# Pinning the first matmul of each recurrence and level step behind the matmul emitted just ahead of it

## The chip, the core and the metric

The kernel runs on one core of one Trainium2 chip. A core has five engines with a queue each, worked off in order: PE (matmuls, with its weight loads shown apart as PEld), DVE, ACT and POOL for elementwise work, and SP, which issues nearly all DMAs here. The metric is the device time of one execution in microseconds, as the median of several runs. Before the change the three runs took 3159.82, 3169.68 and 3175.28 us.

## What is computed

Two layers of a backbone over 256 latent and 256 context tokens, 2048 channels wide. The first layer is a bidirectional gated DeltaNet, the second a differential attention. Each is wrapped in RMSNorm, an adaptive shift, scale and gate, a SiLU gate and an output projection. The change lies in the DeltaNet alone, whose core in the reference is this:

```python
tinv = lax.linalg.triangular_solve(eye + lower, eye, left_side=True, lower=True, unit_diagonal=True)
u = tinv @ (vc * bc[..., None])
w = tinv @ (kb * jnp.exp(gc)[..., None])
...
def step(s, inp):
    q_i, k_i, u_i, w_i, a_i, gl_i = inp
    v_new = u_i - w_i @ s
    o_i = q_i @ s + a_i @ v_new
    s = s * gl_i[..., None, None] + jnp.einsum('bhck,bhcv->bhkv', k_i, v_new)
    return s, o_i
```

There are 16 key heads with two value heads each, in both directions. The steps of the scan depend on each other through the state `s`.

## The kernel before, in words

The 512 tokens are cut into four chunks of 128, and the work of the DeltaNet into 16 groups `g`, one for each key head, with its two value heads `h` and two directions `dd`. For each group these things run:

- **The filler** (`filler`, lines 671 to 696): six input projections (k, q, v0, v1, z0, z1) of 48 matmuls each, 128x512, with weights split in a high and a low part. Their PSUM tiles are called `pj`, and there are two. They don't depend on the recurrence, but what they write does: the tiles `sz` for z0 and z1 exist twice, and are freed when the outputs of a group are finished (`chain_fin`).
- **The levels** (`stream_lev`, lines 779 to 826; two such streams): the triangular inverse of a chunk, doubled in three levels. A level is a matmul group `iv<-T,m`, a mask on DVE that makes `R` (line 807), the group `iv<-U,R`, and, but for the last level, `iv<-R,U` and two copies on ACT (lines 824, 825).
- **The recurrence** (`steps_b`, lines 873 to 957): four steps `t` per group. A step is a chain of PE groups with an elementwise operation behind each: `sb<-S,kT` and then `y` on DVE and its cast `yb` on ACT (895 to 903); `sb<-yb,uf` and the copy `x0` (920, 922); `sb<-x0,m` and the residual `yb` (926 to 929); `sb<-yb,uf` again and `x` (933, 935); `sb<-x,kx` and the state `S` (940 to 946). The outputs are `so<-S,qT` and `so<-x,at` (907, 952).
- Beside them `stream_m` and `stream_at` (decay matrices, and a block inverse in small DVE operations, lines 736 and 738), and the pieces of the adaptive modulation on POOL and ACT.

**Who sets the order.** Two layers do. The class `Drive` (lines 521 to 563) runs these generators against a clock of its own: after each piece a generator yields the PE time it used and the latency until its next piece may be emitted, and the ready one with the lowest priority number goes next (recurrence 1, levels 1.5, the filler 9). This gives the order in which instructions are emitted. Then the framework's scheduler sets the order on each engine, by a model of when each instruction is ready: an instruction may be put ahead of ones that were emitted earlier on its engine. What it decides is fixed when the program is built; on the chip each engine takes its queue in that order.

After the loop the output projection follows in two halves of heads, tiles `woA0` to `woA15` (heads 0 to 15) and `woB0` to `woB15` (heads 16 to 31), 48 matmuls each; a head's output goes through the DRAM tensor `yd` and is loaded again as `yr`, then split into `yh` on ACT (204) and `yl` on DVE (206). The second layer comes last. All calls of `mm` appear in the profile as line 87.

Of the kernel before, what the change touches and what calls it, by code (L numbers as in the profile page):

```python
# [20 lines left out]
P = 128  # L21
# [44 lines left out]
def body(ctx, tc, D, d, out):  # L66
    nc = tc.nc
# [16 lines left out]
    wp = ctx.enter_context(pool("wp", side="right"))  # L84

    def mm(o, l, r, start=True, stop=True):
        nc.tensor.matmul(o, l, r, start=start, stop=stop)  # L87

    cs = cst.tile([P, C_MAIN], F32, name="cs")
    nc.sync.dma_start(cs, d["consts"][:, :C_MAIN])  # L90
# [182 lines left out]
    def sb():  # L273
        return psm.tile([P, 2, 2, P], F32, tag="sb", name="sb", bufs=1)

    def so():
        return psm.tile([P, 2, 2, P], F32, tag="so", name="so", bufs=1)
# [43 lines left out]
    for k0 in range(0, KT, SK):  # L321
# [12 lines left out]
        for n, src, _ in EARLY:  # L334
            w = SK * P
            r = t0.tile([P, w], F32, tag="er", name=f"e{n}r{k0}", bufs=4)
# [178 lines left out]
    def ev(*k):  # L515
        return evs.setdefault(k, Event())
# [48 lines left out]
    dr = Drive()  # L565
    LX = 1.8

    def free(k, n=1, lat=0.0):
        if lat:
            dr.add(0, later(k, n), lat)  # L570
        else:
            res[k].free += n

    def later(k, n):
        res[k].free += n
        return
        yield
# [120 lines left out]
    def quad(t):  # L698
        return t.rearrange("p (u i) -> p u i", u=4)
# [79 lines left out]
    def stream_lev(p):  # L779
        yield ev("conv", 0, "v0")  # L780
        yield ev("conv", 0, "v1")
        for g in range(G):
            for half in range(2):
                yield ev("tu", g, half)
                yield ("uf", 1)
                st = sts[g]
                c = 2 * half + p
                m16 = st["m"][half][0]
                tu = st["tu"][half]

                def t16(tag):
                    return dl.tile([P, 4, P], F16, tag=f"{tag}{p}", name=f"{tag}{g}{c}", bufs=1)

                lvb = lambda n: lv[:, n - 4].unsqueeze(1).to_broadcast([P, 4, P])
                Tm, U = t16("T"), t16("U")
                for dst, src in ((Tm, tu[0]), (U, tu[1])):
                    for dd in range(2):
                        nc.sync.dma_start(dst[:, 2 * dd:2 * dd + 2], src[p, :P, dd])
                dr.set("ld", g, half, p)
                yield 0.0, 4.0  # L800
                for n in range(4, 7):
                    last = n == 6
                    pp = iv()
                    for u in range(4):
                        mm(pp[:, u * P:(u + 1) * P], m16[:, u // 2, p, u % 2], Tm[:, u])
                    R = t16("R")
                    nc.vector.tensor_tensor(R, quad(pp), lvb(n), ALU.mult)  # L807
                    yield 0.22, 30 / 10
                    pu = iv()
                    for u in range(4):  # L810
                        mm(pu[:, u * P:(u + 1) * P], R[:, u], U[:, u])
                    if last:
                        uf = dl.tile([P, 4, P], F16, tag="uf", name=f"uf{g}{c}", bufs=8)
                        nc.scalar.copy(uf, quad(pu))
                        st.setdefault("uf", {})[c] = uf
                        yield 0.22, 1.5 * LX
                        dr.set("uf", g, c)
                    else:
                        U2 = t16("U")
                        pt = iv()  # L820
                        for u in range(4):
                            mm(pt[:, u * P:(u + 1) * P], U[:, u], R[:, u])
                        U, Tm = U2, t16("T")
                        nc.scalar.copy(Tm, quad(pt))  # L824
                        nc.scalar.copy(U, quad(pu))  # L825
                        yield 0.43, 30 / 10
# [46 lines left out]
    def steps_b(g, t, half, st, S, O):  # L873
        kT, qT, ktok, uf = st["kT"], st["qT"], st["ktok"], st["uf"]
        v = st["v"][half]
        m16, ml = st["m"][half]
        cd = (ORDER[0][t], ORDER[1][t])
        col = lambda a, dd, h: a[:, cd[dd], dd, 2 * g + h:2 * g + h + 1]
        fl = lambda a: a.rearrange("p d h i -> p (d h i)")
        f2 = lambda a: a.rearrange("p h i -> p (h i)")  # L880
        DH = [(dd, h) for dd in range(2) for h in range(2)]

        def vec(tag, dt=F32):
            return dl.tile([P, 2, 2, P], dt, tag=tag, name=f"{tag}{g}{t}", bufs=1)

        if t < 3:
            kx = vec("kx")
            for dd in range(2):
                nc.gpsimd.tensor_tensor(kx[:, dd], ktok[:, cd[dd]].unsqueeze(1).to_broadcast([P, 2, P]),
                                        kd[:, cd[dd], dd, 2 * g:2 * g + 2].unsqueeze(2).to_broadcast([P, 2, P]),  # L890
                                        ALU.mult)
        if t > 0:
            b = sb()
            for dd in range(2):
                mm(f2(b[:, dd]), kT[:, cd[dd]], f2(S[:, dd]))
            y = vec("y")
            for dd, h in DH:
                nc.vector.scalar_tensor_tensor(y[:, dd, h], b[:, dd, h], col(eg, dd, h), v[:, cd[dd] % 2, h],
                                               ALU.mult, ALU.subtract)
        else:  # L900
            y = v
        yb = vec("yb", BF16)
        nc.scalar.copy(fl(yb), fl(y))
        if t > 0:
            o1 = so()
            for dd in range(2):
                mm(f2(o1[:, cd[dd] % 2]), qT[:, cd[dd]], f2(S[:, dd]))
            for dd, h in DH:
                c = cd[dd] % 2
                if t == 2:  # L910
                    nc.scalar.activation(O[:, c, h], o1[:, c, h], AF.Copy, scale=col(eg, dd, h))
                else:
                    nc.vector.scalar_tensor_tensor(O[:, c, h], o1[:, c, h], col(eg, dd, h), O[:, c, h],
                                                   ALU.mult, ALU.add)
            yield 1.7, 2.6 * LX
        else:
            yield 0.0, 1.0 * LX
        b = sb()
        for dd, h in DH:
            mm(b[:, dd, h], uf[cd[dd]][:, 2 * dd + h], yb[:, dd, h])  # L920
        x0 = vec("x0", BF16)
        nc.scalar.copy(fl(x0), fl(b))
        yield 0.22, 1.6 * LX
        b = sb()
        for dd, h in DH:
            mm(b[:, dd, h], m16[:, dd, cd[dd] % 2, h], x0[:, dd, h], True, False)
            mm(b[:, dd, h], ml[:, dd, cd[dd] % 2, h], x0[:, dd, h], False, True)
        rb = vec("yb", BF16)
        nc.vector.tensor_tensor(fl(rb), fl(y), fl(b), ALU.subtract)  # L929
        yield 0.43, 1.8 * LX  # L930
        b = sb()
        for dd, h in DH:
            mm(b[:, dd, h], uf[cd[dd]][:, 2 * dd + h], rb[:, dd, h])
        x = vec("x")
        nc.vector.tensor_tensor(fl(x), fl(x0), fl(b), ALU.add)  # L935
        yield 0.22, 1.8 * LX
        if t < 3:
            b = sb()
            for dd, h in DH:
                mm(b[:, dd, h], kx[:, dd, h], x[:, dd, h])  # L940
            if t == 0:
                nc.vector.tensor_copy(fl(S), fl(b))
            else:
                for dd, h in DH:
                    nc.vector.scalar_tensor_tensor(S[:, dd, h], S[:, dd, h], col(egl, dd, h), b[:, dd, h],
                                                   ALU.mult, ALU.subtract)
        if t % 2 == 0:
            yield ev("at", g, half)
        at = st["at"]
        o0 = so()  # L950
        for dd, h in DH:
            mm(o0[:, cd[dd] % 2, h], at[cd[dd]][:, 2 * dd + h], x[:, dd, h])
        if t == 0:
            nc.scalar.copy(fl(O), fl(o0))
        else:
            nc.vector.tensor_tensor(fl(O), fl(O), fl(o0), ALU.subtract)
        yield (1.74 if t < 3 else 0.87), (2.2 if 0 < t < 3 else 1.0) * LX
# [93 lines left out]
    for ct in range(KT):  # L1051
        ps = pj()
        wout_tile(ps, d["wout"][0, ct], f"woA{ct}", yA, T, True, True)
        x = dl.tile([P, T], F32, tag="th", name=f"xb{ct}", bufs=2)
# [94 lines left out]
    for p in range(NP_):  # L1149
# [12 lines left out]
        for hd in range(2):  # L1162
            dh = 2 * p + hd
            spread(late_1, dh, KT // 2, 4)
            qT, kT = [], []
# [17 lines left out]
            for qt in range(2):  # L1183
# [30 lines left out]
                o = l1.tile([P, 256], F32, tag="lo", name=f"lo{dh}{qt}", bufs=2)  # L1214
# [90 lines left out]
def build(nc, arrays, D):  # L1305
    d = {n: nc.dram_tensor(f"in_{n}_dram", a.shape, mybir.dt.from_np(a.dtype), kind="ExternalInput").ap()
         for n, a in arrays.items()}
    out = nc.dram_tensor("out_0_dram", (P, D // P, 256), F32, kind="ExternalOutput").ap()
    with tile.TileContext(nc, schedule_with_timeline_sim=True) as tc:
        body(tc, D, d, out)  # L1310
# [12 lines left out]
```

## Time and profile before

| | |
|---|---|
| median of three runs | 3169.68 us (3159.82 to 3175.28) |
| the profiled execution | 3178.9 us |
| its span, first to last instruction | 3177.1 us |
| PE busy | 2847.2 us, 90% |
| DVE, POOL, ACT busy | 66%, 66%, 59% |
| mean granted TensorE clock | 0.956 |

The span is that of the profiled execution, 1.8 us less than its time. From 250 to 2000 us the groups of the DeltaNet run, with the same mix of work all along; before it lie the first norm and the first projections, behind it the output projection and the second layer. Busy time of PE is modelled from the length of each matmul, so the idle time and the spacing of starts say more than the busy share. The clock is a share of full speed: 1.0 is 2.4 GHz and 0.5 is 1.2 GHz, the only two levels.

### The profile page before, as it was taken

The page shows a single profiled execution, that of the slowest core. Times are in us where ns is not written, and L with a number is a line of the kernel's source. Part 1 is how long each engine was busy: PE and PEld are TensorE (multiplying, and loading weights), DVE is VectorE, ACT ScalarE, POOL GpSimd, SP SyncE. Part 2 cuts the span into 40 slices and gives each one's busy share as a digit, 9 for nine tenths or more (in the row PEclk, how much of TensorE's full clock was granted, in tenths as well). Part 3 has the DMA queues.
Part 4 walks back from the last instruction along what each step waited for, and adds up shares of the span by engine and source line. Part 5 has one row for each costly group of instructions (what it writes and reads, how often), then busy time and mean ns, then how long its engine had stood idle before and what let it go on. Part 6 is the DMA issues. An engine that isn't in the chain of part 4 may idle for free.

```text
span 3177.1 us, 51834 instructions
## 1 busy us (share of the span) xinstructions
PE 2847.2 (90%) x15822; PEld 2245.4 (71%) x15822; DVE 2108.5 (66%) x4475; ACT 1863.0 (59%) x5447; POOL 2086.8 (66%) x2370
## 2 busy tenths in 40 slices
PE   7777898888988988988988988899898999999998
PEld 3455676666766766766766766678686888888897
DVE  7978868768688688688688677632334654544454
ACT  4245666666766766666665765654455665634354
POOL 5877677776777777677777767566466666722234
PEclk8888999999999999999999999899999999999999
DMA  9634445555545445445455455666754555533335
GB/s 336 237 99 117 119 126 126 129 128 127 133 124 133 127 127 138 119 122 136 128 120 139 124 127 123 168 176 198 221 149 126 152 156 158 155 114 110 115 128 163
DMA packets 507183, 457.01 MB, mean 144 GB/s; under 512 B 241171, under 2 KB 383251, under 8 KB 502803
## 3 DMA queue, kind: packets, MB, share of 16 engines
q1 hardware_dynamic: 506900, 453.68, 51.4%
q8 instruction: 124, 2.03, 0.3%
q14 instruction: 157, 1.29, 0.2%
q10 hardware_dynamic: 2, 0.02, 0.0%
HBM read 427.18 MB, written 26.36 MB: 143 GB/s over the span
## 4 chain that ended last, share of the span: by engine, by line
PE 27%; DVE 11%; DMA 10%; POOL 5%; ACT 4%; issue 4%; SPq 1%; POOLq 0%; DVEq 0%; ACTq 0%
PE pj L87 24%; POOL rp L149 3%; DMA aw<-in_adaw_dram 3%; DMA gra<-gc_d 2%; DMA grm<-gc_d 2%; DVE bP L736 1%; DVE gra L711 1%; DVE grm L711 1%; ACT rp L150 1%; PE at L87 1%; PE sb L87 1%; PE iv L87 1%; DVE bY L738 1%; DMA yr<-yd 1%; DVE R L807 0%
## 5 line engine op out<-in xcount | busy, mean ns | idle before, releaser
L150 ACT ACTIVATE rp<-rp 128x256 f32<-128x256 f32 x1024 | 426.6, 417 | 397.9 <-POOL rp L149 394.0
L736 DVE TENSOR_TENSOR bP<-bX,bY 64x1 f32<-64x1 f32 (+14 forms) x480 | 226.2, 471 | 12.3 <-ACT bY L734 4.7
L150 ACT ACTIVATION_READ_ACCUMULATOR rp<-rp 128x1 f32 x1024 | 193.8, 189 | 0.0
L711 DVE TENSOR_SCALAR grm<-grm,gct,lnb 128x128 f32<-128x128 f32 x256 | 140.5, 590 | 63.3 <-DMA grm<-gc_d 62.6
L711 DVE TENSOR_SCALAR gra<-gra,gct,lnb 128x128 f32<-128x128 f32 x256 | 117.1, 500 | 84.1 <-DMA gra<-gc_d 83.6
L807 DVE TENSOR_TENSOR R<-iv,lv 128x512 f16<-128x512 f32 x192 | 127.0, 679 | 44.4 <-PE iv L87 44.0
L166 DVE CUSTOM_DVE_ANT_0 aj<-ar,crow 128x1024 bf16<-128x1024 f32 x80 | 116.1, 1452 | 10.7 <-DMA ar<-in_adaw_dram 9.5
L87 PEld LDWEIGHTS <-m 128*128 128x128 f16 x1024 | 75.8, 101 | 60.8 <-issue 53.2
L713 ACT ACTIVATE grm<-grm 128x512 f32<-128x512 f32 x64 | 40.3, 630 | 130.3 <-DVE grm L711 130.1
L738 DVE TENSOR_REDUCE bY<-bP 64x1 f32<-64x1 f32 (+14 forms) x480 | 108.8, 227 | 8.4
L769 POOL TENSOR_TENSOR ma<-ma,cs 128x512 f32<-128x512 f32 x64 | 86.2, 1346 | 24.4 <-DVE ma L719 14.8
L87 PE MATMUL iv<-U,R 128*128 128x128 f16 x768 | 76.1, 225 | 22.7 <-DVE R L807 18.6
L87 PEld LDWEIGHTS <-R 128*128 128x128 f16 x768 | 48.2, 100 | 65.2 <-DVE R L807 29.9
L713 ACT ACTIVATE gra<-gra 128x512 f32<-128x512 f32 x64 | 40.3, 630 | 84.8 <-DVE gra L711 81.4
L87 PE MATMUL iv<-T,m 128*128 128x128 f16 x768 | 73.5, 227 | 17.9 <-DMA T<-tu_d 13.1
L87 PE MATMUL sb<-yb,uf 128*128 128x128 bf16 x512 | 54.5, 225 | 39.1 <-DVE yb L929 24.0
L87 PEld LDWEIGHTS <-uf 128*128 128x128 f16 x512 | 35.4, 101 | 67.4 <-issue 59.4
L772 POOL TENSOR_TENSOR ml<-ma,m 128x512 bf16<-128x512 f32 x64 | 75.1, 1174 | 7.8 <-ACT m L771 7.7
L824 ACT CAST T<-iv 128x512 f16<-128x512 f32 x128 | 73.8, 577 | 7.8 <-PE iv L87 6.8
L87 PE MATMUL so<-x,at 128*128 128x128 f32 x512 | 74.1, 281 | 2.1 <-DVE x L935 1.8
L825 ACT CAST U<-iv 128x512 f16<-128x512 f32 x128 | 75.6, 591 | 0.0
L87 PEld LDWEIGHTS so<-x,at 128*128 128x128 f32 x512 | 66.9, 195 | 4.2 <-DVE x L935 2.2
(2767 smaller groups left out, 11567.0 us busy)
## 6 DMA issues: line engine op xcount, KB each, us to landing
aw<-in_adaw_dram SPq DMA_DIRECT2D x512, 128.0 KB, 3.0
ar<-in_adaw_dram SPq DMA_DIRECT2D x32, 1024.0 KB, 6.1
gra<-gc_d SPq DMA_DIRECT2D x128, 128.0 KB, 4.4
grm<-gc_d SPq DMA_DIRECT2D x128, 128.0 KB, 4.3
mb_d<-m SPq DMA_DIRECT2D x32, 256.0 KB, 4.5
U<-tu_d SPq DMA_DIRECT2D x128, 64.0 KB, 2.7
T<-tu_d SPq DMA_DIRECT2D x128, 64.0 KB, 2.4
yd<-sz SPq DMA_DIRECT2D x32, 256.0 KB, 2.9
```

Source lines behind the costliest of these rows:

```text
L87: nc.tensor.matmul(o, l, r, start=start, stop=stop)
L149: nc.gpsimd.tensor_tensor(pr, r, cr[:, s], ALU.mult)
L150: nc.scalar.activation(pr, pr, AF.Copy, accum_out=acc[:, s, q:q + 1])
L166: nc.vector.tensor_tensor_reduce(jk, rq, cr, 1.0, 0.0, ALU.mult, ALU.add, a)
L711: nc.vector.tensor_scalar(gr[:, u], gr[:, u], gct[:, c, dd, j:j + 1], lnb[:, c, dd, j:j + 1], ALU.subtract, ALU.min)
L713: nc.scalar.activation(gr, gr, AF.Exp)
L736: nc.vector.tensor_tensor(pr[:, :i, :i], X[:, i, :i].unsqueeze(1).to_broadcast([64, i, i]), Y[:, :i, :i].rearrange("p j c -> p c j"), ALU. ...
L738: nc.vector.tensor_reduce(Y[:, i, :i], pr[:, :i, :i], AX.X, ALU.add)
L769: nc.gpsimd.tensor_tensor(ma, ma, ident.unsqueeze(1).to_broadcast([P, 4, P]), ALU.add)
L772: nc.gpsimd.tensor_tensor(ml[:, :, k], mv, m16[:, :, k], ALU.subtract)
L807: nc.vector.tensor_tensor(R, quad(pp), lvb(n), ALU.mult)
L825: nc.scalar.copy(U, quad(pu))
```

## The change

`mm` now returns its instruction. A helper `pin` passes the first matmul (`k == 0`) of a PE group to the scheduler's `keep_in_program_order`, which adds an edge of order, without a wait, to the PE instruction emitted just before it. So the scheduler may no longer put this matmul ahead of that one. Instructions emitted later may still go ahead of the pinned one, and the other matmuls of the group have no such edge. In a level the groups `iv<-T,m` and `iv<-U,R` are pinned, in a step `sb<-S,kT`, both `sb<-yb,uf`, `sb<-x0,m` and `sb<-x,kx`.

```diff
     def mm(o, l, r, start=True, stop=True):
-        nc.tensor.matmul(o, l, r, start=start, stop=stop)
+        return nc.tensor.matmul(o, l, r, start=start, stop=stop)
...
+    def pin(k, ins):
+        return tc.keep_in_program_order(ins) if k == 0 else ins
...
-                        mm(pp[:, u * P:(u + 1) * P], m16[:, u // 2, p, u % 2], Tm[:, u])
+                        pin(u, mm(pp[:, u * P:(u + 1) * P], m16[:, u // 2, p, u % 2], Tm[:, u]))
...
-                        mm(pu[:, u * P:(u + 1) * P], R[:, u], U[:, u])
+                        pin(u, mm(pu[:, u * P:(u + 1) * P], R[:, u], U[:, u]))
...
-                mm(f2(b[:, dd]), kT[:, cd[dd]], f2(S[:, dd]))
+                pin(dd, mm(f2(b[:, dd]), kT[:, cd[dd]], f2(S[:, dd])))
...
-            mm(b[:, dd, h], uf[cd[dd]][:, 2 * dd + h], yb[:, dd, h])
+            pin(2 * dd + h, mm(b[:, dd, h], uf[cd[dd]][:, 2 * dd + h], yb[:, dd, h]))
...
-            mm(b[:, dd, h], m16[:, dd, cd[dd] % 2, h], x0[:, dd, h], True, False)
+            pin(2 * dd + h, mm(b[:, dd, h], m16[:, dd, cd[dd] % 2, h], x0[:, dd, h], True, False))
...
-            mm(b[:, dd, h], uf[cd[dd]][:, 2 * dd + h], rb[:, dd, h])
+            pin(2 * dd + h, mm(b[:, dd, h], uf[cd[dd]][:, 2 * dd + h], rb[:, dd, h]))
...
-                mm(b[:, dd, h], kx[:, dd, h], x[:, dd, h])
+                pin(2 * dd + h, mm(b[:, dd, h], kx[:, dd, h], x[:, dd, h]))
```

Two places show what this does to PE's order. The first is in group 9, from the state update of step 0 (`x90`, `kx90`) to the next step's use of the state (`S9`); `g10v0` and `g10z1` are weights of the filler for group 10, `g11q` of that for group 11. PE's rows before:

```order
L87 MATMUL pj_15740<-hhi_100,g10v0hi0256_15794 128x512
L87 MATMUL pj_15740<-hlo2_452,g10v0hi0256_15794 128x512
L87 MATMUL sb_15634<-x90_15601,kx90_15419 128x128 x4
L87 MATMUL so_15650<-x90_15601,at90_15450 128x128 x2
L87 MATMUL so_15650<-x90_15601,at91_15462 128x128 x2
L87 MATMUL pj_15740<-hhi_100,g10v0lo0256_15795 128x512
...
L87 MATMUL sb_15760<-S9_15417,kT9_13708 128x256 x2
L87 MATMUL pj_15740<-hhi_100,g10v0lo1256_15817 128x512
L87 MATMUL pj_15740<-hhi_100,g10v0hi1256_15816 128x512
```

And PE's rows now, from the last filler matmul ahead of the place to the first one behind it:

```order
L87 MATMUL pj_16678<-hhi_100,g10z1lo3256_17015 128x512
...
L87 MATMUL sb_15634<-x90_15601,kx90_15419 128x128 x4
L87 MATMUL so_15650<-x90_15601,at90_15450 128x128 x2
L87 MATMUL so_15650<-x90_15601,at91_15462 128x128 x2
L985 MATMUL so_15750<-cs_63,O81_14787 128x128 x4
L87 MATMUL sb_15760<-S9_15417,kT9_13708 128x256 x2
L87 MATMUL so_15770<-S9_15417,qT9_14277 128x256 x2
...
L595 MATMUL tr_16632<-cs_63,thg11k_16421 128x128 x4
...
L87 MATMUL pj_17046<-hhi_100,g11qhi00_17049 128x512
```

The same step stands four projections later against the filler (behind z1 of group 10, where it stood within v0), and no filler matmul is left between its parts: 56 matmuls stand there without one, from the residual of step 0 to the correction of step 1. The second place is the end of the recurrence: the transposes of the last group's last output (`O151`), which heads 30 and 31 of `woB` wait for. PE's rows before:

```order
L87 MATMUL pj_25857<-yh0_24554,woA8hi00_25860 128x512
L87 MATMUL pj_25857<-yl0_24555,woA8hi00_25860 128x512
L87 MATMUL pj_25857<-yh0_24554,woA8lo00_25861 128x512
L982 MATMUL so_24532<-cs_63,O151_24359 128x128
L87 MATMUL pj_25857<-yh1_24563,woA8hi00_25860 128x512
L982 MATMUL so_24532<-cs_63,O151_24359 128x128 x3
```

And PE's rows now:

```order
L87 MATMUL pj_27085<-yh17_27103,woB0hi00_27088 128x512
L87 MATMUL pj_27085<-yl17_27104,woB0hi00_27088 128x512
L985 MATMUL so_24532<-cs_63,O151_24359 128x128 x3
L87 MATMUL pj_27085<-yh17_27103,woB0lo00_27089 128x512
L985 MATMUL so_24532<-cs_63,O151_24359 128x128
L87 MATMUL pj_27085<-yh18_27112,woB0hi00_27088 128x512
```

They stood in the ninth tile of the first half of the output projection, and stand in the first tile of the second half.

## Rows read from the trace of the kernel before

**Rows 1.** The page, busy time, share of the span and instructions by engine

```profile
PE 2847.2 (90%) x15822; PEld 2245.4 (71%) x15822; DVE 2108.5 (66%) x4475; ACT 1863.0 (59%) x5447; POOL 2086.8 (66%) x2370
```

**Rows 2.** Busy time by stretch: us, engines (instructions), clock, DMA share, GB/s

```profile
core 0: us, PE busy (x) PEld busy (x) DVE busy (x) ACT busy (x) POOL busy (x), PEclk, DMA share, GB/s
250.00:2000.00 1750.00, 1544.78 (x9011) 1190.04 (x9012) 1351.93 (x3117) 1143.43 (x3530) 1286.16 (x1595) 0.96 0.51 127
370.34:381.18 10.84, 8.00 (x64) 6.62 (x64) 10.53 (x27) 7.46 (x22) 3.91 (x6) 0.84 0.24 66
```

**Rows 3.** PE's waits from 250 to 2000 us: total us, times, longest

```profile
PE iv L87 <- DVE R L807: 22.4, 27, 2.7
PE sb L87 <- DVE yb L929: 22.0, 16, 3.4
PE sb L87 <- ACT yb L903: 14.3, 9, 4.8
...
PE iv L87 <- ACT T L824: 7.3, 7, 2.2
PE sb L87 <- DVE x L935: 5.8, 7, 2.2
PE sb L87 <- DVE S L942: 5.7, 5, 1.7
```

**Rows 4.** PE's timeline without filler, group 0: start, duration, [idle before <-releaser]

```profile
370.34 1.13 PE L87 MATMUL sb<-S,kT 128*128 128x256 f32 x4 [0.23 <-DVE S L942]
...
371.67 1.08 PE L87 MATMUL so<-S,qT 128*128 128x256 f32 x4
372.59 0.39 PE L87 MATMUL iv<-R,U 128*128 128x128 f16 x4
375.40 0.38 PE L87 MATMUL sb<-yb,uf 128*128 128x128 bf16 x4 [2.43 <-ACT yb L903]
...
377.53 0.26 PE L87 MATMUL sb<-x,m 128*128 128x128 bf16 x1 [0.21 <-ACT x L922]
...
380.47 0.80 PE L87 MATMUL iv<-U,R 128*128 128x128 f16 x8
381.18 0.50 PE L87 MATMUL pj<-hhi,g2qhi 128*128 128x512 f32 x1
```

**Rows 5.** PE's timeline where a level group interrupts the filler, group 7

```profile
1019.94 0.40 PE L87 MATMUL iv<-R,U 128*128 128x128 f16 x4
1020.15 0.48 PE L87 MATMUL pj<-hlo,g7v1hi 128*128 128x512 f32 x1
1020.47 0.40 PE L87 MATMUL pj<-hhi,g7v1lo 128*128 128x512 f32 x1
1020.70 0.40 PE L87 MATMUL pj<-hhi,g7v1hi 128*128 128x512 f32 x1
```

**Rows 6.** DVE's groups by form: busy us, mean ns | idle before, releaser

```profile
L711 DVE TENSOR_SCALAR grm<-grm,gct,lnb 128x128 f32<-128x128 f32 x256 | 140.5, 590 | 63.3 <-DMA grm<-gc_d 62.6
L898 DVE SCALAR_TENSOR_TENSOR y<-sb,eg,v 128x128 f32<-128x128 f32 x192 | 54.3, 339 | 11.4 <-PE sb L87 11.2
L719 DVE TENSOR_TENSOR ma<-grm,gm 128x512 f32<-128x512 f32 x64 | 52.1, 814 | 5.6 <-ACT grm L713 4.5 <-ACT rp L150 0.5
L935 DVE TENSOR_TENSOR x<-x,sb 128x512 f32<-128x512 bf16 x64 | 43.3, 677 | 24.0 <-PE sb L87 23.8
```

**Rows 7.** The reloaded heads: casts, splits, and the DMA from issue to landing

```profile
L204 ACT CAST yh<-yr x32: 602/618/633, 2015.8 to 2263.4; 128x512 fp32r<-128x512 f32 x32
L206 DVE TENSOR_TENSOR yl<-yr,yh x32: 677/692/1226, 2017.5 to 2264.0; 128x512 fp32r<-128x512 f32 x32
...
DMA to landing us min/median/max: 2.6/4.0/6.4
```

**Rows 8.** The page, DMA issues: KB each, median us from issue to landing

```profile
yd<-sz SPq DMA_DIRECT2D x32, 256.0 KB, 2.9
```

## Prediction

> **What bounds the kernel now.** I read the busy line of the page first: PE is the fullest engine with 90%, the others stand at 59 to 66% [rows 1]. But a share over the whole span says little, so the next view is the busy time by stretch. From 250 to 2000 us, where the DeltaNet groups run, PE is busy 1544.8 of 1750 us [rows 2]. So PE sets the pace there, and what is to be won or lost is the other 205 us, and the clock (0.96, so about 140 us run at half speed and some 70 us are lost by it). PE's waits show who ends the idle time: the six largest of the recurrence and the levels on elementwise operations make 22.4 + 22.0 + 14.3 + 7.3 + 5.8 + 5.7 = 77.5 us [rows 3]. The rest is spread over many filler projections, each waiting a little for its split weights. PE takes its queue in order, so a recurrence matmul whose operand is late holds up the filler behind it; what matters is how much filler stands between a step and the next. The timeline shows one place where none does: from 370.34 to 381.18 us, in group 0 [rows 4].
>
> **What the change moves.** It adds no instruction and no wait on a semaphore, only edges of order, on 672 matmuls (384 in levels, 288 in the recurrence). Whether it moves anything is read off PE's new order, and it moves much, as the two places beside the diff show. Counted over the DeltaNet and the first half of the output projection:
> - The filler is cut into 539 runs where it was 674. That is 135 interruptions fewer.
> - Stretches of 24 or more matmuls without one of the filler: 1 before, 14 now, with 28 to 100 matmuls each, 56 in the mean; one or so per group, spread over the groups. The one before has 60, and it is the one in rows 4.
> - The recurrence runs later against the filler, by four projections in group 9. By then z0 and z1 of group 10 hold both `pj` tiles until group 8's output frees `sz`, so there is no filler left to put between the steps.
>
> **What a stretch without filler costs.** Rows 4 hold its price: 10.84 us for 64 matmuls by the trace's count, which takes a float32 matmul as two. At full clock and without waits, the 48 of 16 bits take 0.056 us each (four in 0.21 us from start to start [rows 5]), the eight of 256 float32 columns 0.23 each (from 371.67 to 372.59 [rows 4]), the eight transposes half of that: 2.7 + 1.8 + 0.9 = 5.4 us. So the price is 10.84 - 5.4 = 5.4 us. Its parts: waits of 0.23, 2.43 and 0.21 us, and a clock of 0.84 [rows 2], which is 10.84 x 0.16 x 2 = 3.5 us at half speed and 1.7 us lost; the rest is small gaps. DVE was busy 10.53 of the 10.84 us [rows 2]: in such a stretch the steps wait for DVE's queue, in which their operations stand among the decay and block work.
>
> As a check, the stretch of group 9 in the new order. From its first residual to its second `x`, DVE has six pieces of decay, eight scaled updates (`y`, and `O` taken as long), five whole tiles (two residuals, two `x`, one `S`) and two `ma`: 6 x 0.590 + 8 x 0.339 + 5 x 0.677 + 2 x 0.814 = 11.3 us [rows 6]; three casts on ACT at some 0.6 us stand in the chain with it, so some 13 us. PE has 20 matmuls of 16 bits, 24 float32 passes and 12 transposes of 0.115 and four passes of 0.46, together 7.1 us. That makes 6 us, beside the 5.4.
>
> Bounds: below, the three waits alone, 2.9 us (the clock stays up). Zero is excluded because the chain of six dependent steps can't be shorter than its operations. Above, the whole stretch at half clock, 5.4 + 2.9 = 8.3 us. I take 5.4, the one that was measured. Thirteen more make 13 x 5.4 = 70 us (38 to 108), and the one of group 0 grows from 60 matmuls to 100, 5.4 x 40 / 60 = 4 us.
>
> The row shows the clock at half speed for a third of the stretch. The Trainium skill (TensorE: Matmul & The Clock Gate, Loop structure matters more than you think) says that matmuls stay warm when they stand back to back, and run cold when each waits for something. Held for the whole stretch it would make it 8.3 us and not 5.4, and the sum 38 us larger; the trace agrees with it in part, so it is the upper bound here.
>
> **What is won.** An interruption of the filler costs the longer start of the matmul behind it, 0.32 us (1020.15 to 1020.47) in place of 0.23 (1020.47 to 1020.70) [rows 5]: 0.09 x 135 = 12 us (0 to 12, since behind a float32 group the price may be less). Outside the stretches without filler a step now has somewhat more filler behind it than before. The recurrence's own four waits make 22.0 + 14.3 + 5.8 + 5.7 = 47.8 us [rows 3]; I take a quarter off, 12 us. The bounds are 0 and all 77.5. I stay near the low end because in the levels there is no more filler between the groups than before, and because DVE and ACT answer late whenever their own queue is long, which no edge on PE changes.
>
> **The tail.** The last heads are finished in the first tile of `woB`, where they were finished in the ninth of `woA`. Store, load, cast and split of heads 30 and 31 take 2.9 + 4.0 + 0.62 + 0.69 = 8.2 us [rows 7, 8]. That tile reads them at its 15th of 16 steps of three matmuls; from the transposes that is some 12 steps, 36 x 0.23 = 8.3 us. So it is even, where before it was hidden by half a projection; behind the two stores on SP stand the loads of heads 26 to 31 and a piece of weights, which then come late too. I take 2 us (0 to 6).
>
> **Sum.** 70 + 4 - 12 - 12 + 2 = +52 us. From the profiled execution, 3178.9 us, that is 3231 us; against the median of the runs shown, 3169.7 us, which is 9 us less, **3222 us**. Its own range, with the price between 3.5 and 7.5 us: +20 to +95, 3190 to 3265 us.
>
> **The rivals.**
> - *The stretches are deeper.* DVE's queue is longer than in group 0 or the clock stays at half speed: 108 + 5 - 12 + 6 = +107, 3277 us. For it speaks that DVE was full in the one seen; against it, that ACT and POOL work is nearly absent there and later stretches are shorter on average.
> - *It cancels.* Price as measured, but three quarters of the 77.5 us of waits go: 74 - 12 - 58 + 2 = +6, 3176 us. For it: the waits are many and short (86 in the six rows), and a little more filler behind each could cover them.
> - *Faster.* The place is the waits of rows 3: before, steps stand in PE's queue ahead of filler that could have run, and if the pins end this wholly, 77.5 + 12 us are won. The stretches without filler cost only their three waits, 13 x 2.9 + 2 = 40 us: -77.5 - 12 + 40 + 2 = -48, 3122 us. With all waits gone it is faster as long as a stretch costs less than 6.4 us. Against it: the waits come mostly from late DVE and ACT, and the new order adds the very places where nothing covers them.
> - *The pins do nothing*, since the scheduler would order so anyway. The order excludes it: 135 runs of the filler fewer.
>
> **Chances.** Forecast 0.55, deeper 0.17, cancels 0.15, faster 0.13. About 0.5%, 16 us, is what can be told from no change. So slower 0.72, same 0.15, faster 0.13. The range reaches into the cancelling and the faster case and to the deeper one: 3150 to 3285 us.
>
> **What would show it.** In the new trace, from 250 to 2000 us and somewhat behind, about one stretch per group in which PE has no filler, 8 to 13 us long, with DVE full and the clock under 0.9; PE's idle time in the DeltaNet larger by some 40 us, mostly on `yb`, `x`, `R`, `T` and `y`; the end of the last step in the second half of the output projection. It is wrong if these stretches last little more than their matmuls, if the waits on line 929 and 903 fall to nothing, or if the second half of the output projection waits for its last heads by more than 6 us.

## The result, and the profile after

The changed kernel takes 3209.1 us (median of four runs, 3201.9 to 3217.0). The kernel before, run beside it on the same chip, takes 3172.5 us (3159.8 to 3177.1). The medians lie 37 us apart, where +52 was forecast. The ratio on record is 1.0134, interval 1.0114 to 1.0155, which would be 36 to 49 us, so 37 is at its low end. The profiled execution took 3217.0 us with a span of 3215.2 us, 38.1 us longer than the span before, and the mean granted clock is 0.951 (before 0.956). Lines behind the helper `pin` stand three further down than before: 929 is now 932.

The busy line of the page tells next to nothing. All five shares are within two points of those before, and the count of instructions is the same [rows 1]:

```profile
PE 2863.7 (89%) x15822; PEld 2262.3 (70%) x15822; DVE 2099.4 (65%) x4475; ACT 1871.6 (58%) x5447; POOL 2067.6 (64%) x2370
```

PE's waits from 250 to 2000 us (total us, times, longest) show growth on some lines and none on others:

```profile
PE iv L87 <- DVE R L810: 31.8, 28, 3.7
PE gq L87 <- DVE gm L721: 27.4, 15, 4.6
PE sb L87 <- DVE yb L932: 26.8, 13, 4.7
PE iv L87 <- ACT T L827: 14.6, 11, 2.7
PE sb L87 <- ACT yb L906: 10.1, 11, 3.4
...
PE sb L87 <- DVE x L938: 5.3, 6, 2.2
```

Against [rows 3] `R` grew by 9.4 us, `yb` on 932 by 4.8 and `T` by 7.3, while `yb` on 906 fell by 4.2. The waits on 932 became fewer and longer (13 times, up to 4.7 us). The line `gm`, a DVE operation on the products `gq` of keys and queries that the forecast did not have among its rows, grew most, by 15.4 us, and is now the second. Before, it was this:

```profile
PE gq L87 <- DVE gm L718: 12.0, 12, 3.0
```

The places that the forecast counted in PE's order are there in the trace. From 250 to 2250 us PE has 14 stretches of 32 or more matmuls without filler, 206.5 us long together, from 5.9 to 29.5 us each; seven of them lie within the 8 to 13 us that were forecast. Busy time by stretch (the whole DeltaNet, then the stretch of group 9, then the last and longest one):

```profile
core 0: us, PE busy (x) PEld busy (x) DVE busy (x) ACT busy (x) POOL busy (x), PEclk, DMA share, GB/s
250.00:2000.00 1750.00, 1538.28 (x8803) 1189.97 (x8803) 1300.17 (x3003) 1141.71 (x3537) 1293.68 (x1624) 0.95 0.51 127
1419.59:1439.38 19.79, 10.85 (x74) 8.90 (x73) 15.18 (x33) 11.14 (x34) 13.53 (x17) 0.83 0.52 124
2011.10:2040.58 29.48, 15.02 (x108) 12.04 (x108) 23.20 (x47) 22.71 (x60) 13.72 (x16) 0.79 0.62 169
```

In group 9 the stretch lasts 19.79 us where the forecast's estimate came to 13, and PE is busy for little more than half of it. Its timeline on PE (start, duration, and in brackets the idle time before it and what ended it):

```profile
1419.35 0.40 PE L87 MATMUL pj<-hhi,g10z1lo 128*128 128x512 f32 x1
1419.59 0.23 PE L87 MATMUL sb<-x,m 128*128 128x128 bf16 x1
...
1420.05 0.66 PE L87 MATMUL gq<-kT 128*128 128x128 f32 x4
1425.44 0.58 PE L87 MATMUL sb<-yb,uf 128*128 128x128 bf16 x4 [4.74 <-DVE yb L932]
1426.81 2.08 PE L87 MATMUL sb<-x,kx 128*128 128x128 f32 x8 [0.78 <-DVE x L938]
...
1434.01 1.10 PE L87 MATMUL so<-S,qT 128*128 128x256 f32 x4 [0.91 <-DVE sz L988]
1435.60 0.38 PE L87 MATMUL sb<-yb,uf 128*128 128x128 bf16 x4 [0.49 <-ACT yb L906]
...
1437.28 0.22 PE L87 MATMUL sb<-x,m 128*128 128x128 bf16 x1 [0.74 <-ACT x L925]
...
1439.38 0.50 PE L87 MATMUL pj<-hhi,g11qhi 128*128 128x512 f32 x1
```

And DVE's timeline over the wait of 4.74 us:

```profile
1420.35 2.99 DVE L714 TENSOR_SCALAR gra<-gra,gct,lnb 128x128 f32<-128x128 f32 x4 [1.64 <-DMA gra<-gc_d]
1423.27 1.53 DVE L714 TENSOR_SCALAR grm<-grm,gct,lnb 128x128 f32<-128x128 f32 x4
1424.72 0.67 DVE L932 TENSOR_TENSOR yb<-v,sb 128x512 bf16<-128x512 f32 x1
```

The residual `yb` has its PSUM operand soon after 1420.0. But in DVE's queue eight pieces of decay stand ahead of it, and the first of them is itself held until its load has landed. So the step is answered at 1424.72. Its own operation takes 0.67 us; the rest of the wait is queue.

**Where the 38 us of the span went.** For each stretch I took its length less what its matmuls take at full clock, as the forecast did for [rows 4]; that is its price. Outside I summed PE's idle time ahead of its instructions and the time at half clock (half of which is lost), all from 250 to 2250 us:

| us | before | after | difference |
|---|---|---|---|
| price of the stretches without filler | 5.4 (1) | 122.6 (14) | +117 |
| PE idle, outside of them | 216.9 | 158.8 | -58 |
| at half clock, outside of them | 154.7 | 115.1 | -40, so 20 less lost |
| sum | | | +39 |

The window is equally long in both, so the sum says how much less of the work fits into it. The mean price is 122.6 / 14 = 8.8 us, from 1.6 us to 21. About two thirds of it is waits (83 us, 7 of them ahead of the filler matmul behind a stretch); the rest is the clock, which was at half speed for 79 of the 206.5 us and so lost 40.

### The profile page after: what moved, and what is told of

The parts are those of the page before. It is cut to its first block, busy times and chain, and to the rows that moved or that the text cites. A ratio compares the mean times of both kernels' runs of the same rounds, so it can differ in the third digit from the quotient of the medians.

```text
span 3215.2 us, 51930 instructions
## 1 busy us (share of the span) xinstructions
PE 2863.7 (89%) x15822; PEld 2262.3 (70%) x15822; DVE 2099.4 (65%) x4475; ACT 1871.6 (58%) x5447; POOL 2067.6 (64%) x2370
## 5 line engine op out<-in xcount | busy, mean ns | idle before, releaser
L714 DVE TENSOR_SCALAR grm<-grm,gct,lnb 128x128 f32<-128x128 f32 x256 | 132.7, 561 | 53.5 <-DMA grm<-gc_d 53.2
L722 DVE TENSOR_TENSOR at<-gra,gm 128x512 f32<-128x512 f32 x64 | 53.2, 832 | 39.9 <-PE so L87 38.2
```

The costliest lines, as they stand in the source:

```text
L714: nc.vector.tensor_scalar(gr[:, u], gr[:, u], gct[:, c, dd, j:j + 1], lnb[:, c, dd, j:j + 1], ALU.subtract, ALU.min)
```

## The experiments

Each was timed beside the kernel before on the same chip. Two theories stood first. **Theory A**: each stretch costs its 8.8 us, and the pins otherwise save some 80 us by themselves, so pins that make no stretch should win. **Theory B**: what is saved outside is only what other engines catch up on while PE gives time away.

The table has for each kernel its ratio to the kernel before with the interval, the stretches (32 or more matmuls without filler), the matmuls that stand in them, their mean price, and PE's idle time for 100 matmuls that aren't filler, inside and outside the stretches. The last five columns are worked out from PE's timeline of one execution each, 250 to 2250 us.

| | ratio | stretches | matmuls in them | price, us | idle inside | idle outside |
|---|---|---|---|---|---|---|
| before | 1 | 1 | 64 | 5.4 | 4.8 | 2.9 |
| after | 1.0134 [1.0114, 1.0155] | 14 | 908 | 8.8 | 8.4 | 2.6 |
| e1 | 1.0027 [1.0012, 1.0041] | 1 | 96 | 9.6 | 6.4 | 3.1 |
| e2 | 1.0101 [1.0084, 1.0117] | 15 | 876 | 7.9 | 8.9 | 2.3 |
| e3 | 1.0003 [0.9993, 1.0013] | 1 | 96 | 9.1 | 6.2 | 2.7 |
| e4 | 1.0207 [1.0189, 1.0226] | 6 | 404 | 8.3 | 7.4 | 2.7 |
| e7 | 1.0155 [1.0133, 1.0178] | 3 | 128 | 1.7 | 2.3 | 3.3 |
| e8 | 1.0053 [1.0034, 1.0072] | 9 | 536 | 7.2 | 7.4 | 2.7 |
| e9 | 1.0306 [1.0285, 1.0327] | 1 | 68 | 5.5 | 4.3 | 2.8 |
| e10 | 1.0088 [1.0068, 1.0109] | 15 | 953 | 6.9 | 6.9 | 2.7 |
| e11 | 0.9998 [0.9982, 1.0014] | 1 | 52 | 4.8 | 5.1 | 2.8 |
| e6 | 0.9767 [0.9742, 0.9793] | 1 | 64 | 5.8 | 5.2 | 2.2 |
| e5 | 0.9852 [0.9836, 0.9869] | 12 | 744 | 8.0 | 8.4 | 1.9 |
| e12 | 0.9491 [0.9469, 0.9512] | 8 | 520 | 6.2 | 5.9 | 0.8 |

**e1, e2, e3: parts of the change.** e1 pins the levels alone (one of the five edits, the others are alike):

```diff
-                pin(dd, mm(f2(b[:, dd]), kT[:, cd[dd]], f2(S[:, dd])))
+                mm(f2(b[:, dd]), kT[:, cd[dd]], f2(S[:, dd]))
...
```

> Only the levels' groups are pinned, the recurrence is free again. PE's order has 1 stretch without filler (84 matmuls) and 603 filler runs. Theory A (the time of the change is the stretches without filler, some 8.8 us each, less what the pins save elsewhere, about 80 us): no stretches, part of the saving stays, so faster than before by 10 to 40 us, 3130 to 3160. Theory B (what is saved elsewhere is only work that the other engines catch up on while PE stands in the stretches; pins save nothing of themselves): no stretches and no saving, within 15 us of before.

e2 pins the recurrence alone (the group `iv<-U,R` is edited likewise):

```diff
-                        pin(u, mm(pp[:, u * P:(u + 1) * P], m16[:, u // 2, p, u % 2], Tm[:, u]))
+                        mm(pp[:, u * P:(u + 1) * P], m16[:, u // 2, p, u % 2], Tm[:, u])
...
```

> Only the recurrence's groups are pinned, the levels are free again. PE's order has 15 stretches without filler, of 28 to 78 matmuls, 49 in the mean, and 516 filler runs. Both theories: as slow as the full change or somewhat less, 3195 to 3220 us; a time near the kernel before (under 3185) would say that the pins on the levels matter as much and neither theory has the cause.

e3 pins only where the matmul emitted just ahead is one of the filler:

```diff
...
-        return tc.keep_in_program_order(ins) if k == 0 else ins
+        return tc.keep_in_program_order(ins) if k == 0 and fil[1] else ins
...
```

> The same groups are pinned, but only where the matmul emitted just ahead is one of the filler; inside the emitted stretches the scheduler is free. PE's order has 1 stretch without filler (84 matmuls) and 617 filler runs, and the last step stands in the ninth tile of the first half of the output projection, as before. Theory A: 50 to 80 us faster than the kernel before less the longer first stretch, 3100 to 3135 us. Theory B: within 15 us of before.

Measured: e1 3176.2, e2 3199.7, e3 3168.8 us, beside 3167.0 for the kernel before. The pins of the levels cost 9 us (4 to 13 by the interval), though they add no stretch and only make the one longer, from 64 to 96 matmuls, at 4 us; those of the recurrence cost 33, and the stretches come with them. Pins without stretches win nothing, though e1 and e3 cut the filler into 603 and 617 runs in place of 674. Theory A falls.

**e4 and e7: a shorter assumed latency.** `LX` scales the latency until a step's next piece may be emitted. e4 has it at 1.4 with all pins, e7 without any:

```diff
-    LX = 1.8
+    LX = 1.4
```

> All pins of the change, and the factor LX on the planner's latencies 1.4 in place of 1.8, so that the recurrence is emitted earlier. PE's order has 5 stretches without filler (48, 42, 108, 50 and 46 matmuls) where the change has 14, 554 filler runs. Theory A: 5 stretches cost some 45 us in place of 123, the rest stays: 3125 to 3150 us. Theory B: the saving shrinks with the stretches, 3172 + 37 x 5/14, 3180 to 3190 us.

> The kernel before with the assumed latency of a step at 1.4 and no pin, the base for e4; one stretch without filler. If the shorter latency alone is what made e4 slow (steps are emitted before their operands are there): 3205 to 3235 us. If it was the pins: 3155 to 3180 us, and the pins then cost 55 us or more with only six stretches, so that the count of stretches does not carry their price.

e4 fitted neither theory: 3233.6 us with only six stretches. e7 says why. It takes 3214.4 us (before 3165.9), so the latency alone costs 48 us, and the pins on top of it some 18. Without e7 one would have laid all of e4's 67 us to the pins. But the 18 us come with three stretches more in the trace, so 6 us each (4.5 by PE's order, which has four more), about twice the net cost of the comparisons below. Why is open, and that cost holds only for the planner's latency as it was.

**e8: nine stretches.** All pins but those on `sb<-S,kT`, which opens a step:

```diff
-                pin(dd, mm(f2(b[:, dd]), kT[:, cd[dd]], f2(S[:, dd])))
+                mm(f2(b[:, dd]), kT[:, cd[dd]], f2(S[:, dd]))
```

> All pins but those of the product of the state with the keys, which opens a step: 9 stretches without filler (24 to 126 matmuls) in place of 14, 592 runs of filler. If the time goes with the matmuls that stand in such stretches (470 here, 784 in the changed kernel, and 37 us there): plus 15 to 30 us, 3182 to 3197. If it goes with the pins and not with the stretches: within 8 us of the changed kernel, 3196 to 3212 us. If it goes with neither: within 8 us of the kernel before.

3183.4 us beside 3165.9: +17.5, as expected if the time goes with the matmuls in such stretches. Divided by the stretches added, the net cost is 36.6 / 13 = 2.8 us for the whole change, 32.7 / 14 = 2.3 for e2, and 17.5 / 8 = 2.2 here (by the ratios 3.3, 2.3 and 2.1).

**e9: PE made busy by other means.** No pin, but 32 more filler matmuls in each group:

```diff
+                        if kind == "z0" and kt == 0:
+                            for j in range(32):
+                                mm(ps, hi[:, ks], hh(j % KT), j == 0, j == 31)
                         mm(ps, hi[:, ks], hh(kt), kt == 0, False)
```

> The kernel before (no pin) with 32 more matmuls 128x512 ahead of the first one of each z0 projection, whose sum the real first matmul overwrites: 16 x 32 x 0.233 = 119 us more work for PE at full clock, about as much as the 14 stretches without filler cost in the changed kernel (117 us). Theory B, what the pins save outside the stretches is only that DVE, ACT and the loads catch up while PE gives time away: the gaps of PE outside shrink here as well, by 40 to 80 us, and the kernel is 40 to 80 us slower than before (ratio 1.013 to 1.025). Rival, the saving comes from the order itself, since pinned steps have more filler behind them: extra work can't bring it, and the kernel is 100 to 119 us slower (1.032 to 1.038).

3264.5 us beside 3166.5: 98 of the 119 us are paid, 21 come back (16 to 29 by the interval), between the two forecasts and nearer to the rival's. So Theory B holds for about a fifth. This extra work isn't a stretch, though: it adds none (the table has one, as before), and the clock from 250 to 2000 us is 0.97, before 0.96. Its busy time by stretch:

```profile
250.00:2000.00 1750.00, 1562.11 (x9052) 1215.78 (x9053) 1277.28 (x2961) 1128.53 (x3537) 1288.56 (x1605) 0.97 0.50 126
```

So neither theory explains the 78 us that are saved outside the stretches (58 of idle time, 20 of clock). About half of it is not saved at all, but moved. In both traces PE's matmuls of each name are equally many, so the 844 that stand in the added stretches can be found again in the trace before, as the same ones in the order of their name. There PE idled 36.7 us ahead of them (4.35 us for 100, where the mean is 2.93) and ran 7.5 us around them at half clock. This time is no longer counted outside: these steps waited before as well, and now wait 73.2 us inside, twice as long. In e2 and e8 beside the kernel before, e5 beside e6 and e10 beside e11 the moved waits come to 38, 22, 34 and 34 us in the same way. The other matmuls that aren't filler wait nearly as before, 110.6 us ahead of 4180 and now 106.8 ahead of 4156, so the fall of the last column from 2.9 to 2.6 is almost all a change of the mix. The filler's own waits outside fell from 69.6 to 51.9 us. 36.7, 3.7 and 17.7 make the 58.

**e5, e6, e12: what a stretch waits for.** The trace of group 9 suggests the loads of the decay rows (`gra` and `grm`). e5 (with all pins) and e6 (without) leave these loads out, and the decay pieces read a resident tile:

```diff
...
-        for dd in range(2):
-            nc.sync.dma_start(gr[:, 2 * dd:2 * dd + 2, :],
...
-            nc.vector.tensor_scalar(gr[:, u], gr[:, u], gct[:, c, dd, j:j + 1], lnb[:, c, dd, j:j + 1],
+            nc.vector.tensor_scalar(gr[:, u], ident, gct[:, c, dd, j:j + 1], lnb[:, c, dd, j:j + 1],
```

> The changed kernel without the loads of the decay rows (DVE's decay piece reads a resident tile instead; the same count of DVE instructions, wrong decay values, 13 stretches without filler in PE's order, 24 to 76 matmuls long). Theory C, what makes a stretch dear is a decay piece at the head of DVE's queue that waits for its own load: the mean price of a stretch falls from 8.8 to under 6 us, DVE is over 90% busy inside the stretches, and the time lies within 15 us of the same edit of the kernel before (e6). Theory D, the price is the step's own chain from engine to engine and the clock that falls in it: price 7.5 to 9.5 us, and e5 is slower than e6 by 28 to 45 us, as the changed kernel is than the kernel before.

> The kernel before, without the loads of the decay rows in the same way; one stretch without filler, as before. It is the base for e5. Theory C: 5 to 25 us faster than the kernel before, since the waits of DVE for these loads (84 us in the stretch from 250 to 2000 us) hold up steps there too, though mostly under filler. Theory D: within 10 us of the kernel before.

e5 takes 3119.3 and e6 3093.5 us beside 3165.9. Without the loads the kernel before is 72 us faster, more than either theory had (the 84 us in the expectation of e6 are the waits for `gra` alone; with `grm` they are 144). But the difference between pinned and unpinned is 25.8 us with 11 stretches added, 2.3 each, a little under what Theory D had; and the price of a stretch is 8.0 us, not under 6. Theory C's price is not reached. Busy time by stretch in two stretches of e5:

```profile
911.50:933.39 21.89, 11.44 (x74) 9.19 (x73) 20.25 (x41) 14.10 (x45) 15.72 (x18) 0.84 0.33 89
1140.20:1162.18 21.98, 11.85 (x74) 9.39 (x73) 18.73 (x36) 12.36 (x38) 14.72 (x17) 0.84 0.34 80
```

DVE is now busy for 152.2 of the 169.8 us in its stretches (90%). In the changed kernel it was busy for 154.2 of 206.5 (75%), the sum of its 14 stretches:

```profile
sum 206.51, PE 128.69 PEld 104.56 DVE 154.21 ACT 135.06 POOL 111.46; mean PE 9.19 PEld 7.47 DVE 11.02 ACT 9.65 POOL 7.96
```

It stood for another 30.4 us within them before a piece whose load hadn't landed (19.8 for the decay rows, the rest for `bk` of the block inverse): 89% together. For each matmul a stretch lasts 0.228 us in the one and 0.227 in the other, so without the loads a stretch was not shorter. But the edit did more than it was meant to: DVE's pieces of `grm` in the stretches take 738 ns in e5 (57 pieces) and 432 in the changed kernel (44). That is 57 x 0.306 = 17.4 us more, or 1.5 us for each of the 12 stretches, as much as the waits that are gone, 19.8 / 14 = 1.4 us. So e5 doesn't show that the loads are without weight. e12 takes the work away too (in the kernel with all pins; the diff is against e5):

```diff
...
-        for u in range(4):
...
-            nc.vector.tensor_scalar(gr[:, u], ident, gct[:, c, dd, j:j + 1], lnb[:, c, dd, j:j + 1],
-                                    ALU.subtract, ALU.min)
-        nc.scalar.activation(gr, gr, AF.Exp)
+        nc.scalar.activation(gr, ident.unsqueeze(1).to_broadcast([P, 4, P]), AF.Exp)
```

> The changed kernel with neither the loads of the decay rows nor DVE's four operations for each of them (ACT's exponential reads a resident tile; wrong decay values); 8 stretches without filler, 34 to 64 matmuls. In e5 the loads were gone and a stretch stayed as dear (0.228 us and 0.084 us of waits for each matmul in it, as in the changed kernel), with DVE busy 90% of it. If it is DVE's work that a stretch waits for: with some 18% less of it, PE waits under 0.06 us for each matmul in the stretches, these cost under 6 us each, and DVE is under 85% busy in them. If it is the chain of answers from engine to engine, however free DVE is: 0.08 us or more of waits, and 7 us or more each. The time itself, 3040 to 3110 us, tells them not apart, since DVE's work is missing everywhere.

3004.2 us beside 3166.9. Two of its stretches:

```profile
664.70:680.18 15.48, 10.92 (x72) 9.14 (x73) 12.48 (x31) 9.51 (x28) 12.27 (x17) 0.91 0.37 105
877.90:890.80 12.90, 9.54 (x73) 7.76 (x73) 10.15 (x26) 8.92 (x26) 11.76 (x16) 1.00 0.38 105
```

PE idles 0.059 us for each matmul in a stretch (under the 0.06 set, and down from 0.084), the price is 6.2 us (just over the 6 set), DVE is 71% busy, and the clock in the stretches is 0.95, where it was 0.81. So DVE's queue is a good part of the price: for each matmul it falls from 0.135 us in the changed kernel (0.128 in e5) to 0.095. This fits what was taken away: in the changed kernel the decay pieces held DVE for 26.9 us in the stretches and their loads for 19.8, 3.3 us a stretch, and the price fell by 2.6. The other two thirds remain, with DVE idle for over a quarter of the time. How much of them is DVE's remaining work and how much the chain of answers from engine to engine is not told apart.

**e10, e11: a second tile for the decay rows.** Two `grm` in place of one, paid for with a `ktok`; e10 with all pins, e11 without:

```diff
...
-        kt_ = dl.tile([P, NCH, P], F32, tag="ktok", name=f"ktok{g}", bufs=3)
+        kt_ = dl.tile([P, NCH, P], F32, tag="ktok", name=f"ktok{g}", bufs=2)
...
-        gr = dl.tile([P, 4, P], F32, tag=tag, name=f"{tag}{g}{c}", bufs=1)
+        gr = dl.tile([P, 4, P], F32, tag=tag, name=f"{tag}{g}{c}", bufs=2 if tag == "grm" else 1)
```

> The changed kernel with two tiles grm for the decay rows of the levels instead of one (so that a load need not wait until the tile is free), paid for with two ktok tiles instead of three; 15 stretches without filler. If DVE waits for these loads because they start late: 10 to 40 us faster than the changed kernel, and the stretches cheaper by 1 to 2 us each. If they are late for another reason (SP's queue, the load itself): within 10 us of the changed kernel or slower by the missing third ktok.

> The kernel before with the same two grm and two ktok tiles. If the late start of the loads is what DVE waits for: 10 to 40 us faster than the kernel before, so a version that beats both. Against e10 it shows the price of the pins once more: 25 to 45 us by the count of stretches (15), at 2 to 3 us net for each as in e8, e2 and the changed kernel.

e10 3196.8, e11 3166.4 us beside 3166.5. Without pins the second tile brings nothing, where 10 to 40 us were expected. With them it brings some 12 us against the changed kernel (6 to 15 by what each is set against), and the price is 6.9 us, 1.9 less, so the loads do carry a part of it. The difference of e10 and e11 is 30.5 us for 14 stretches, 2.2 each. None of the kernels that do the whole computation beat the kernel before by more than can be measured.

## Why the prediction came out right, and which of its terms were wrong

The sign, the range and the mechanism of the loss were right. That the sum came close was luck: the price of the stretches was 43 us more than forecast (117 for 74), and what is saved outside them 54 us more (78 for 24). No sign of being wrong that the forecast had named came up.

- **The bound.** PE sets the pace, and its waits are the stake: right. PE's idle time from 250 to 2250 us rose by 22 us (219.9 to 242.2), not 40. The forecast laid the idle time beyond its six rows to the filler, which had 69.6 us of it; `gm` was left out, 12.0 us and now 27.4. The six rows of [rows 3] hold 71 waits and not the 86 that the rival "cancels" names.
- **The count, 13 stretches more.** Right, read from the order alone, and in the places named: the recurrence of group 9 stands behind z1 of group 10 with no filler between its steps. e8, e2 and the two pairs (e5 with e6, e10 with e11) show that the cost goes with it, at 2.2 to 2.8 us net each; e4 beside e7 has a higher one. The reason given, that z0 and z1 wait for `sz`, was not tried on the chip. The traces fit it: from 250 to 2000 us filler matmuls wait for `sz` (line 503) 6 times, 6.7 us in all, and once before, 0.6 us.
- **The price, 5.4 us.** Mis-sized: 8.8 us. The term of +74 is +117. The one stretch that could be measured before was a mild one: group 0, with 64 matmuls and a single wait over 0.3 us [rows 4]; of the 14 only two have a lower price (1.6 and 5.0 us). The forecast's own estimate for group 9 came to 13 us, 6 over the matmuls; the trace has 19.79 us there, 12 over, of which DVE waited 3.5 us for loads, which the estimate left out. The upper bound of 8.3 us is passed by the mean, and by the last stretch with 21. It is passed by waits and not by a clock that stays low: 79 of 206.5 us were at half speed. The forecast weighed a rule of the Trainium skill (TensorE: Matmul & The Clock Gate, Loop structure matters more than you think), whose example of matmuls that run cold is a loop with a wait for a DMA before each. With waits for DVE and ACT the trace agrees in part again: the granted clock is 0.81 over the 14 stretches, and 1.00 in two of them.
- **"DVE full".** Right in substance, wrong as a row to look for: DVE is 75% busy in the stretches, and 89% with the time it is held up by a load at the head of its queue. e12 shows that the decay pieces and their loads carry about a third of the price.
- **Interruptions, -12.** Not seen. e1 and e3 have 71 and 57 runs of filler fewer and gain nothing; at 0.09 us each that would be 5 to 6 us. e3's interval leaves room for 2 us at most, unless its pins cost something elsewhere.
- **Waits outside, -12.** Far too small: 58 us of idle time and 20 us of half clock, 78 in all. The reason given, more filler behind a step, is worth 4 us: so much less do the steps wait that stayed outside. The step that failed is the bookkeeping. The forecast charged each new stretch in full and left the waits outside nearly as they were, but the steps in the stretches brought their old waits along (36.7 us, and 3.7 of the clock). The price had to be taken as the surplus over what the same steps waited before.
- **The tail, +2.** Nothing: PE's waits for `yh` from 2200 to 2500 us are 4.7 us with a longest of 1.9, before 6.1 with 2.6.

Of the rivals, "deeper" had nearly the right price (8.3) and "cancels" nearly the right gain outside (58 + 12); both happened at once, the gain for another reason than that rival gave. What stays open is a part of it: of the 78 us, 40 are moved waits and clock, and some 20 may be engines that catch up, if what e9 shows holds here too. The remaining 18 or so, in the filler's waits and the clock, are not explained.

## What to carry to other kernels

A constraint on the order costs where it gathers dependent steps with nothing independent between them: count such stretches in the new order before running it, here 2 to 3 us net each in five comparisons, and about twice that in a sixth. To price one, subtract what its steps waited before, and look at the mean stretch rather than the only one at hand. When a tuning constant is used as a dose, run it without the change too: e4 alone would have misled.

## What had not been expected of the hardware

- The loads of the decay rows, 128 KB each and some 4 us from issue to landing, cost 72 us of 3166 (e6), though DVE's pieces took 50 us more without them. That is half of the 144 us that DVE waits for them from 250 to 2000 us in the kernel before (62.6 for `grm` [rows 6] and 81.1 for `gra`, the line below). DVE's work on them costs another 115 us (e12 against e5, both pinned, with 8 stretches in place of 12).

```profile
DVE gra L711 <- DMA gra<-gc_d: 81.1, 63, 4.4
```

- In e5 and e6 the same operation of DVE became longer when its input no longer came by a load: the pieces of `grm` took 759 and 749 ns in the mean, 590 before. Why is open. In e5 and e6, from 250 to 2000 us:

```profile
L709 DVE TENSOR_SCALAR grm<-cs,gct,lnb 128x128 f32<-128x128 f32 x252 | 178.3, 759 | 1.0
L706 DVE TENSOR_SCALAR grm<-cs,gct,lnb 128x128 f32<-128x128 f32 x252 | 175.6, 749 | 0.6
```

- The granted clock was at half speed for 79 of the 206.5 us of the stretches (38%), and outside them for 115.1 of 1793 us (6%), before 154.7 of 1989 (8%). In e12, with less to wait for, it was 0.95 even within the stretches.
